# A two-layer hybrid step on one core: norm rows spread one product later, pools that wait by tile, and the samples' queries on four column tiles of 32 rows

## The chip, the cores and the metric

The kernel runs on one core of a Trainium2 chip. The metric is the device time of one execution in microseconds, the median of several runs. The engines are PE (TensorE), DVE (VectorE), ACT (ScalarE), POOL (GpSimd) and SP (SyncE, which only issues transfers here).

## The reference

One step of a two-layer model for a prompt of 1024 tokens and for 8 samples of 8 new tokens each, which share the weights (1088 columns in all), with D = 1024:

```python
for l in range(2):
    h = rmsnorm(x, g_mix[l])
    if l == 0:   # 8 forget-gate heads of 64, 4 differential heads of 2 x 64
        y = attention(h)   # prompt: causal; sample: 2048 cached positions, gathered by a page table, and its 8 new ones
    else:
        y = lru_mixer(h)
    x = x + y
    h = rmsnorm(x, g_ffn[l])
    x = x + (gelu(conv(h @ wa)) * (h @ wb)) @ wd      # inner size 3072
y = rmsnorm(x, g_final)
# softmax of a sample: fox  q.k/8 + cq - ck        (8 heads)
#                      diff (p1 - lam * p2) @ v    (4 heads, two maps each)
```

All is float32. Dense products are split into high and low parts (three products in the type fp32r); the attention products of a sample and the prompt's value products run in plain float32. An rmsnorm scales a column (a token) by one number, the reciprocal root of its mean square; the kernel computes it per column and has to spread it over all 128 partitions.

## The kernel before, in words

Activations lie with features on partitions and tokens along the free dimension. The program is written stage by stage; a scheduler orders each engine's instructions by program order and by a timeline that it models, so an instruction may go ahead of an earlier one that is not ready. Only in the attention stage is the order of SP's transfers that of the program (`manual_schedule`).

**Projections** (`proj_chunk`, `proj_v`): query, key and value products. The last part, `proj_v`, is merged with the first 24 steps of the samples' attention.

**Attention.** `merge` interleaves two job lists: the prompt's (`unit_scores`, `unit_norm`, `unit_values`) and the samples' (`key_job`, `softmax_job`, `value_job`). For each sample there are eight key jobs and eight value jobs, and each loads two pages (2 x 512 KB) into one of five buffers `raw` (`RAW = 5`), issued by SP at L818. A key job multiplies zero-padded queries `wz` (128 x 64 per chunk c of two heads and per kind, fox or diff) with the keys: eight calls (L858) that write rows 0 to 63 (fox) or 64 to 127 (diff) of a bank. So scores stand in 128 rows: 64 rows fox, head by head, then 64 rows diff, map by map. A value job multiplies the transposed weights `pT` with the values: for each page one call per kind with 512 columns (L932). `end` (L937) scales the sum, and `end_sum` transposes it in four pieces (L944) and picks each head's columns. In the profile each of these plain float32 calls leaves two matmul records, so L858 has 1024 and L932 544.

**Pools.** A pool that is allocated where released ones lay waits until the whole of them is done, unless it is made by `new_pool`, which waits tile by tile. In the first half of the kernel (`attp`, `proj`, `projn`, `vev`, `evp`, `xp`, `flp`, `flc`, `wos`, `rop`, `sa1`, `sa`, `pr`, `pq`, `pa`) they are of the first kind.

**From a mixer to the feed-forward part** (`to_ffn`, called twice). `down` is the output product by Strassen-like sums; its last loop runs over the two column halves c of the second 544 columns: product `t1`, `over` (squares into `hacc`, L1107 and L1108), `end(0)` when c is 0, product `b22`, `over`, `end(1 + c)`. `end(u)` takes the norm's numbers of unit u in `row`: `rstd_cols` sums the squares over partitions on PE (L196) and runs three Newton steps on DVE (L199, L167 to L175, twelve small instructions), then `row_bcast` (PE transposes, L213, and an ACT copy, L1118) spreads them. `half1` scales and splits the operands of the first 544 columns (`b11`, `b21`), `half2` those of one quarter (`t1`, `t2`, `t3`, `t4`, `b22`: 44 DVE instructions). `next(up)` starts `ffn_up`, whose first part multiplies 12 weight chunks with `b11` and `b21` alone (L1211 to L1213, 24 records for each chunk and operand). L1366 to L1368 are the products of `down`, L136 the low parts of all splits.

Of the kernel before, what the change touches and what calls it, by code (L numbers as in the profile page):

```python
# [20 lines left out]
D = 1024  # L21
# [17 lines left out]
STB = 4  # L39
FINE = False  # L40
LEAD = 1
WRAW = 6
# [36 lines left out]
def hybrid_step(ctx: ExitStack, tc: tile.TileContext, xT, w_in, w_fl, w_v, w_out, w_gate, w_x, w_lout, w_ai, ffn_a, ffn_b,  # L79
# [220 lines left out]

    attp = tc.alloc_tile_pool(name="attp", bufs=1, side="right")
    qs = attp.tile([128, 2, 4, TS], F32, name="qs")
# [13 lines left out]
    def attention_consts():  # L316
        SP.dma_start(ptt, ptab)
        SP.dma_start(newm, cst[:, CST["newm"][0]:CST["newm"][1]])
        lamp = tc.alloc_tile_pool(name="lamp", bufs=1, side="right")
# [43 lines left out]
    open_w("wp0", 2, 2)  # L363
    proj = tc.alloc_tile_pool(name="proj", bufs=1)
    projn = tc.alloc_tile_pool(name="projn", bufs=1, side="right")
    vev = tc.alloc_tile_pool(name="vev", bufs=3)
    evp = tc.alloc_tile_pool(name="evp", bufs=2)

# [25 lines left out]
    n0 = Norm(proj, projn, [vcol("mixg", k) for k in range(KC)], V)  # L394
    xp = tc.alloc_tile_pool(name="xp", bufs=1)
    xs = [xp.tile([128, T], F32, name=f"xs{k}") for k in range(KC)]
# [14 lines left out]
    P0 = n0.pairs()  # L411
    flp = tc.alloc_tile_pool(name="flp", bufs=1)
    wfr = flp.tile([128, KC, H], F32, name="wfr")
# [6 lines left out]
    def cached_gates():  # L420
        flc = tc.alloc_tile_pool(name="flc", bufs=1)

# [130 lines left out]
    for h in range(H):  # L553
        SP.dma_start(cqc[h * NQ:h * NQ + NQ, :], bass.AP(tensor=cq_sc.tensor, offset=cq_sc.offset + h * TS, ap=[[1, NQ], [NQ, NB]]))
    S.copy(csel[0:16], csr)
    for i in range(2):
# [3 lines left out]
    cached_gates()  # L560
    wos = tc.alloc_tile_pool(name="wos", bufs=1)
    for j in range(4):
# [9 lines left out]
    wos.release()  # L572
    rop = tc.alloc_tile_pool(name="rop", bufs=1)
    cost = rop.tile([128, T], F32, name="cost")
# [219 lines left out]
    open_ps("psS", "right", ss=4)  # L794
    sa1 = tc.alloc_tile_pool(name="sa1", bufs=1, side="right")
    sa = tc.alloc_tile_pool(name="sa", bufs=2, side="right")

# [27 lines left out]
    def batch_start(bt):  # L825
        b = bt["b"]
        w = bt["w"] = wz[b % 2]
        for kind in range(2):
            for hp in range(2):
                rows = slice(hp * 64, hp * 64 + 64)  # L830
                o, step = (hp * 8, 80) if kind == 0 else (hp * 32, 72)
                S.copy(sub_ap(w[rows], kind * 256 + o, [[step, 4], [1, NQ]]), qs[rows, kind, :, b * NQ:(b + 1) * NQ])
# [33 lines left out]
    def softmax_job(bt):  # L866
        def new_keys():
            b, w, sx, mx = bt["b"], bt["w"], bt["sx"], bt["mx"]
            ps = bt["pn"] = bank("ss")
            bq = slice(b * NQ, (b + 1) * NQ)  # L870
            PE.matmul(ps[:, 0:NQ], csel, cmn[:, bq], start=True, stop=False, skip_group_check=True)
            for c in range(4):
                for kind in range(2):
                    PE.matmul(ps[64 * kind:64 * kind + 64, 0:NQ], w[:, kind, c, :], kn[:, kind, c, bq], start=False,
                              stop=(c == 3), skip_group_check=True)

# [18 lines left out]
    def value_job(bt, g, x):  # L895
# [27 lines left out]
        def mm():  # L923
            if x == 0 and late:
                turn()
            if g == 0 and x == 0:
                bt["po"] = bank("oo")
            pT, po = bt["pT", g], bt["po"]
            for jj in range(n2):
                for kind in range(2):  # L930
                    f = slice(64 * kind, 64 * kind + 64)
                    PE.matmul(po[f], pT[:rows, 2 * x + jj, f], jb["raw"][:rows, jj, kind],  # L932
                              start=(g == 0 and x == 0 and jj == 0), stop=(g == 4), skip_group_check=True)

        def end():
            bt["ob"] = sa.tile([128, 512], F32, name="ob", bufs=2)
            S.activation(bt["ob"], bt["po"], AF.Copy, scale=bt["rl"])  # L937

        def end_sum():
            b, ob = bt["b"], bt["ob"]  # L940
            bq = slice(b * NQ, (b + 1) * NQ)
            pt = bank("tt", (128, 4, 128))
            for c in range(4):
                PE.transpose(pt[:, c, :], ob[:, c * 128:(c + 1) * 128], ident)  # L944
            for hp in range(2):
                rows = slice(hp * 64, hp * 64 + 64)
                V.tensor_copy(mixs[rows, :, bq], sub_ap(pt[rows], hp * 8, [[144, 4], [1, NQ]]))
            V.tensor_reduce(ods[:, :, bq], sub_ap(pt, 64, [[136, 4], [1, NQ], [32, 2]]), axis=AX.X, op=OP.add)
        return [load] + [None] * (LEAD - 1) + [start] + [None] * (GAP - 1) + [mm] + ([end, end_sum] if g == 4 else [])

# [53 lines left out]
    with tc.manual_schedule(engines={SP.engine}):  # L1004
# [3 lines left out]
        close_w()  # L1008
        pr = tc.alloc_tile_pool(name="pr", bufs=1, side="right")
        pq = tc.alloc_tile_pool(name="pq", bufs=1)  # L1010
        pa = tc.alloc_tile_pool(name="pa", bufs=1)
        mrow = pq.tile([128, 512], F32, name="mrow", bufs=1)
# [79 lines left out]
    class UnitNorm:  # L1092


        def __init__(self, pool, pool2):
            self.pool, self.pool2, self.acc, self.count = pool, pool2, {}, {}

# [12 lines left out]
        def row(self, u):  # L1110
            s0, m = UNITS[u]
            nt = 5 if u == 0 else 3
            cols = rstd_cols(self.acc[u], nt, 1.0 / D)
# [5 lines left out]
            row_bcast(cols, nt, evac)  # L1119
            return rb  # L1120
# [81 lines left out]
    def ffn_up(l, ops, uv):  # L1202
# [134 lines left out]

    def down(src, act, sm, nj, x, dp, rp, done, end):

# [72 lines left out]
        for c in two:  # L1412
# [22 lines left out]
    def to_ffn(l, src, act, sm, nj, x_src):  # L1435
# [18 lines left out]
        def end(u):  # L1454
            nonlocal rest1
            if u == 0:
                ops.half1(x, g, nf.row(0))
            else:
                r = nf.row(u)
                if u == 2:  # L1460
                    nfp.release()
                    dp.release()
                    rp.release()
                    rest1 = new_pool(name=f"opr{l}1")
                    ops.open(1, rest1)
# [4 lines left out]
        down(src, act, sm, nj, x, dp, rp, done, end)  # L1470
        xpool.release()
# [318 lines left out]
```

## Time and profile before

| | |
|---|---|
| median of 3 runs | 3138.46 us (3134.02 to 3145.78) |
| the profiled execution | 3136.24 us, its span 3134.5 us |
| PE busy in the span | 2957.0 us (94%), 21141 matmuls |
| DVE busy | 2100.7 us (67%) |
| ACT busy | 1324.4 us (42%) |
| mean granted PE clock | 0.972 |
| moved | 646.96 MB, 206 GB/s |

Times in views count from the start of the span. A row of a timeline gives start and length of a group of instructions of one kind, in brackets the idle time of the engine before it and what ended that. A row of windows gives each engine's busy time and, in parentheses, its instructions, then the granted PE clock as a share of 2.4 GHz, the mean busy share of the 16 DMA engines and what they moved. A matmul's length holds its fill and drain, so lengths of neighbours overlap.

### The profile page before, as it was taken

What the parts mean: (1) busy time and instruction counts of PE and PEld (TensorE: products, weight loads), DVE (VectorE), ACT (ScalarE), POOL (GpSimd) and SP (SyncE); (2) the same over time, 40 slices, a digit from 0 to 9 for tenths busy, and PEclk for the clock granted to TensorE, in tenths of its full rate; (3) what the DMA queues carried; (4) which work ended last, traced back from release to release, by engine and by line L of the source; (5) the groups of instructions that cost most, each with busy time, mean ns of one, the idle gap of its engine ahead of it and who ended that gap; (6) DMA issues with size and microseconds to landing.
All of it is one profiled execution on the core that took longest, in us unless ns stands there. A gap on an engine that the chain in (4) does not pass through costs nothing. (4 is left out here: it accounts for less than half of the span.)

```text
span 3134.5 us, 58133 instructions
## 1 busy us (share of the span) xinstructions
PE 2957.0 (94%) x21141; PEld 2709.5 (86%) x21141; DVE 2100.7 (67%) x4435; ACT 1324.4 (42%) x2477; POOL 398.9 (13%) x817
## 2 busy tenths in 40 slices
PE   7989999999997899899999999999969999999997
PEld 6988856565577899899999999999969899999997
DVE  6563134443458679988856777768785998886567
ACT  4111234444445533343344555555454334344444
POOL 0100010000000112321200011211011222221000
PEclk8999999999998999999999999999979999999999
DMA  4878688898785456544586652325735664448566
GB/s 147 238 226 308 208 324 306 308 338 319 274 263 191 161 174 207 199 143 140 175 269 193 216 184 96 100 97 167 262 126 172 221 209 161 151 145 260 181 187 212
DMA packets 383473, 646.96 MB, mean 206 GB/s; under 512 B 40305, under 2 KB 210690, under 8 KB 381138
## 3 DMA queue, kind: packets, MB, share of 16 engines
q1 hardware_dynamic: 321234, 478.65, 47.6%
q0 software_dynamic: 41792, 141.52, 12.2%
q10 hardware_dynamic: 20160, 23.07, 2.2%
q8 instruction: 166, 2.72, 0.4%
q14 instruction: 121, 0.99, 0.1%
HBM read 476.15 MB, written 166.95 MB: 205 GB/s over the span
## 5 line engine op out<-in xcount | busy, mean ns | idle before, releaser
L1060 ACT CAST b_hi<-b_raw 128x512 fp32r<-128x512 f32 (+1 forms) x645 | 394.8, 616 | 599.7 <-PE mm L1367 236.7
L136 DVE TENSOR_TENSOR b_lo<-b_raw,b_hi 128x512 fp32r<-128x512 f32 (+1 forms) x645 | 439.0, 683 | 236.6 <-ACT b_hi L1060 231.8
L1367 PE MATMUL mm<-d_lo,b_hi 128*128 128x272 f32 x1848 | 526.3, 293 | 4.6 <-DVE d_lo L136 4.5
L1368 PE MATMUL mm<-d_hi,b_lo 128*128 128x272 f32 x1848 | 525.2, 293 | 0.0
L1366 PE MATMUL mm<-d_hi,b_hi 128*128 128x272 f32 x1848 | 479.5, 297 | 40.7 <-ACT d_hi L1360 31.7
L1366 PEld LDWEIGHTS mm<-d_hi,b_hi 128*128 128x128 f32 x1848 | 331.4, 195 | 46.5 <-ACT d_hi L1360 40.6
L1367 PEld LDWEIGHTS mm<-d_lo,b_hi 128*128 128x128 f32 x1848 | 356.5, 193 | 6.4 <-DVE d_lo L136 6.2
L1368 PEld LDWEIGHTS mm<-d_hi,b_lo 128*128 128x128 f32 x1848 | 355.1, 193 | 0.0
L136 DVE TENSOR_TENSOR d_lo<-d_raw,d_hi 128x544 fp32r<-128x544 f32 (+1 forms) x297 | 175.5, 594 | 56.4 <-ACT d_hi L1360 55.2
L1360 ACT CAST d_hi<-d_raw 128x544 fp32r<-128x544 f32 (+1 forms) x297 | 160.8, 543 | 106.4 <-DMA d_raw<-a_b 50.0
L1082 PE MATMUL mm<-hh,b_hi 128*128 128x364 f32 (+1 forms) x480 | 158.5, 331 | 3.7 <-ACT b_hi L1060 3.1
L1083 PE MATMUL mm<-hl,b_hi 128*128 128x364 f32 (+1 forms) x480 | 157.6, 330 | 0.0
L1084 PE MATMUL mm<-hh,b_lo 128*128 128x364 f32 (+1 forms) x480 | 151.3, 330 | 0.0
L160 PE MATMUL mm<-hh,w_hi 128*128 128x364 f32 (+1 forms) x384 | 127.9, 335 | 14.4 <-DVE ev L296 7.9
L932 PE MATMUL oo<-raw,pT 128*64 128x512 f32 (+1 forms) x544 | 138.6, 604 | 1.1 <-ACT pT L921 1.1
L1211 PE MATMUL mm<-b22h,b_hi 128*128 128x272 f32 x384 | 115.0, 299 | 24.4 <-DVE bt L1294 24.4
L858 PE MATMUL ss<-raw,wz 128*64 128x256 f32 x1024 | 137.4, 389 | 0.0
L1271 ACT ACTIVATE ft<-ft 128x544 f32<-128x544 f32 x96 | 63.9, 666 | 169.1 <-DVE ft L1270 168.9
L161 PE MATMUL mm<-hl,w_hi 128*128 128x364 f32 (+1 forms) x384 | 127.9, 335 | 1.6 <-DVE hl L254 1.6
L162 PE MATMUL mm<-hh,w_lo 128*128 128x364 f32 (+1 forms) x384 | 127.3, 333 | 0.0
L675 ACT ACTIVATE st<-st,nb 128x128 f32<-128x128 f32 (+7 forms) x128 | 98.1, 768 | 55.2 <-DVE nb L669 29.4
L1212 PE MATMUL mm<-b22l,b_hi 128*128 128x272 f32 x384 | 114.1, 297 | 0.0
(401 smaller groups left out, 8401.6 us busy)
## 6 DMA issues: line engine op xcount, KB each, us to landing
raw<-in_kc SPq DMA_DIRECT2D x128, 512.0 KB
raw<-in_vc SPq DMA_DIRECT2D x128, 512.0 KB
b_raw<-w_sum SPq DMA_DIRECT2D x174, 256.0 KB
b_raw<-in_ffn_d SPq DMA_DIRECT2D x168, 256.0 KB
b_raw<-in_ffn_a SPq DMA_DIRECT2D x144, 256.0 KB
a_t<-ts POOLq DMA_DIRECT2D x116, 272.0 KB, 4.0
b_raw<-in_ffn_b SPq DMA_DIRECT2D x96, 256.0 KB
d_raw<-a_t SPq DMA_DIRECT2D x87, 272.0 KB
```

The source lines that it names most:

```text
L136: (eng or V).tensor_tensor(out, x, hi, op=OP.subtract)
L160: PE.matmul(ps[:, :n], hi[:, k, :], rh[:, s:s + n], start=(k == order[0]), stop=False)
L858: PE.matmul(ps[64 * kind:64 * kind + 64], w[:, kind, c, :], jb["raw"][:, :, kind, c, :], start=False, stop=(c == 3), skip_group_check=True)
L932: PE.matmul(po[f], pT[:rows, 2 * x + jj, f], jb["raw"][:rows, jj, kind], start=(g == 0 and x == 0 and jj == 0), stop=(g == 4), skip_group_ ...
L1060: S.copy(hi, raw)
L1082: PE.matmul(ps[:, :n], hi, rh[:, s:s + n], start=(k == order[0]), stop=False)
L1083: PE.matmul(ps[:, :n], hi, rl[:, s:s + n], start=False, stop=False)
L1084: PE.matmul(ps[:, :n], lo, rh[:, s:s + n], start=False, stop=(k == order[-1]))
L1360: S.copy(rh, raw)
L1366: PE.matmul(p, wh[:, m, :], rh[:, s], start=(start and j == 0), stop=False, skip_group_check=True)
L1367: PE.matmul(p, wh[:, m, :], rl[:, s], start=False, stop=False, skip_group_check=True)
L1368: PE.matmul(p, wl[:, m, :], rh[:, s], start=False, stop=(j == nj - 1), skip_group_check=True)
```

## The change

1. `UnitNorm.row` is cut into `rms` (sums and Newton steps) and `spread` (transposes and copy). In `to_ffn`, `end(u)` takes `rms(u)`; unit 0 is spread (and `half1` done) in `end(1)`, unit 1 in `mid`, a new call between `t1` and `b22` of c = 1, and unit 2 in `end(2)` after a first part of `ffn_up`, which now yields after chunks 0 to 2 as well. The last norm of the kernel still takes `row`.
2. The pools named above are made by `new_pool`.
3. The samples' queries are laid out by chunk c in 32 rows (two fox heads of 8 rows, then one diff head's two maps of 8). `wz` is 128 x 32 per chunk and kind. A key job still has eight calls of 256 columns, each on 32 columns of the array; a value job has four calls of 256 columns for each page in place of two of 512. The sum is 256 columns wide and takes two transposes, not four. The constants `csel`, `cqc` and `lamc` follow the new rows; `lamc` is filled by four transfers of POOL in place of one DVE copy.

```diff
-        V.tensor_copy(lamc[96:128, 1:2], lamc[96:128, 0:1])
+        for c in range(4):
+            r = slice(32 * c + 24, 32 * c + 32)
+            G.dma_start(lamc[r, 1:2], lamc[r, 0:1])
...
-        t = sa1.tile([128, 2, 4, 64], F32, name=f"wz{i}")
+        t = sa1.tile([128, 2, 4, 32], F32, name=f"wz{i}")
...
-            for c in range(4):
-                for kind in range(2):
-                    PE.matmul(ps[64 * kind:64 * kind + 64], w[:, kind, c, :], jb["raw"][:, :, kind, c, :], start=False,
-                              stop=(c == 3), skip_group_check=True)
+            for kind in range(2):
+                for c in range(4):
+                    PE.matmul(ps[32 * c:32 * c + 32], w[:, kind, c, :], jb["raw"][:, :, kind, c, :], start=False,
+                              stop=(kind == 1), tile_position=(0, 32 * c), skip_group_check=True)
...
-                for kind in range(2):
-                    f = slice(64 * kind, 64 * kind + 64)
-                    PE.matmul(po[f], pT[:rows, 2 * x + jj, f], jb["raw"][:rows, jj, kind],
+                for c in range(4):
+                    f = slice(32 * c, 32 * c + 32)
+                    PE.matmul(po[f, 0:256], pT[:rows, 2 * x + jj, f], jb["raw"][:rows, jj, :, 128 * c:128 * c + 128],
...
-            for c in range(4):
-                PE.transpose(pt[:, c, :], ob[:, c * 128:(c + 1) * 128], ident)
+            for kind in range(2):
+                PE.transpose(pt[:, kind, :], ob[:, kind * 128:(kind + 1) * 128], ident)
...
-        pr = tc.alloc_tile_pool(name="pr", bufs=1, side="right")
+        pr = new_pool(name="pr", bufs=1, side="right")
...
+            if f == NCOV:            # NCOV = 2, in ffn_up's first loop
+                yield
...
             if c == 0:
                 end(0)
+            elif mid:
+                mid()
             product("b22", ps, False, (c,))
...
         def end(u):
             nonlocal rest1
-            if u == 0:
-                ops.half1(x, g, nf.row(0))
-            else:
-                r = nf.row(u)
-                if u == 2:
...
-                    next(up)
-                ops.half2(x, g, r, u - 1)
+            if u == 1:
+                ops.half1(x, g, nf.spread(0))
+            nf.rms(u)
+            if u == 2:
...
+                next(up)
+                ops.half2(x, g, nf.spread(2), 1)
+                next(up)
+
+        def mid():
+            ops.half2(x, g, nf.spread(1), 0)
```

## Rows read from the trace of the kernel before

**Rows 1.** Windows of the whole kernel by engine: the samples' jobs beside `proj_v` (285 to 400 us), and beside the prompt's attention (400 to 898 us).
```profile
285.00:400.00 115.00, 115.00 (x893) 91.47 (x893) 10.77 (x25) 21.59 (x39) 1.46 (x3) 1.00 0.69 249
400.00:898.00 498.00, 494.48 (x3060) 293.23 (x3059) 205.52 (x842) 217.58 (x496) 38.25 (x87) 0.99 0.86 310
```

**Rows 2.** Groups of instructions by line, the whole run: records, busy us, mean ns of one.
```profile
L932 PE MATMUL oo<-raw,pT 128*64 128x512 f32 (+1 forms) x544 | 138.6, 604 | 1.1 <-ACT pT L921 1.1
L858 PE MATMUL ss<-raw,wz 128*64 128x256 f32 x1024 | 137.4, 389 | 0.0
```

**Rows 3.** The same by line for 400 to 900 us.
```profile
L932 PE MATMUL oo<-raw,pT 128*64 128x512 f32 (+1 forms) x496 | 127.2, 604 | 1.1 <-ACT pT L921 1.1
L858 PE MATMUL ss<-raw,wz 128*64 128x256 f32 x800 | 108.9, 390 | 0.0
```

**Rows 4.** Timeline of PE around the first key job.
```profile
285.53 0.28 PE L493 MATMUL tt<-w_hi,hh 128*128 128x256 f32 x1
285.65 0.28 PE L494 MATMUL tt<-w_lo,hh 128*128 128x256 f32 x1
285.86 1.95 PE L858 MATMUL ss<-raw,wz 128*64 128x256 f32 x16
287.74 0.39 PE L495 MATMUL tt<-w_hi,hl 128*128 128x256 f32 x1
```

**Rows 5.** The same timeline cut to 0.03 us (285.85 to 285.88): the records of that job which run in this stretch.
```profile
285.86 0.44 PE L858 MATMUL ss<-raw,wz 128*64 128x256 f32 x2
```

**Rows 6.** The lines of key and value products, 400 to 898 us: shortest, median and longest record in ns, first and last start.
```profile
L858 PE MATMUL ss<-raw,wz x800: 379/379/689, 400.7 to 849.7; 128*64 128x256 f32 x160
L932 PE MATMUL oo<-raw,pT x496: 587/592/1056, 405.6 to 893.5; 128*64 128x512 f32 x155, 8*64 8x512 f32 x11
```

**Rows 7.** Timeline of PE, one sample's new keys: records of 8 columns.
```profile
314.77 0.64 PE L874 MATMUL ss<-kn,wz 128*64 128x8 f32 x16
```

**Rows 8.** Timeline of PE in the merged stage, around a key job.
```profile
600.32 0.43 PE L714 MATMUL tt<-pf,v 128*64 128x256 f32 x1
600.33 0.43 PE L858 MATMUL ss<-raw,wz 128*64 128x256 f32 x1
600.59 0.38 PE L714 MATMUL tt<-pf,v 128*64 128x256 f32 x1
600.60 2.09 PE L858 MATMUL ss<-raw,wz 128*64 128x256 f32 x15
```

**Rows 9.** Windows in the merged stage in which the transfers were dense: 35 us, and the densest window of 100 us.
```profile
500.00:535.00 35.00, 35.00 (x205) 21.35 (x204) 14.37 (x48) 13.76 (x29) 3.45 (x7) 1.00 1.04 406
...
500.00:600.00 100.00, 99.83 (x618) 59.92 (x617) 43.69 (x180) 45.21 (x104) 9.89 (x22) 1.00 0.93 347
```

**Rows 10.** What SP's queue waited for, 400 to 898 us: us in total, times, longest.
```profile
SPq L818 <- PE ss L858: 94.3, 30, 7.6
SPq L818 <- PE oo L932: 93.8, 37, 12.1
```

**Rows 11.** Windows around the first passage to the feed-forward part, and the whole of both passages.
```profile
980.00:1000.00 20.00, 13.43 (x91) 12.94 (x90) 18.04 (x48) 12.37 (x28) 4.28 (x8) 0.78 0.74 244
1000.00:1020.00 20.00, 9.48 (x53) 8.83 (x53) 18.28 (x47) 9.41 (x22) 1.08 (x2) 0.71 0.11 36
1020.00:1040.00 20.00, 13.33 (x88) 12.47 (x87) 19.12 (x50) 11.37 (x28) 3.22 (x6) 0.89 0.43 141
...
1060.00:1080.00 20.00, 20.00 (x162) 20.00 (x162) 11.31 (x24) 12.81 (x29) 4.18 (x11) 1.00 0.69 220
...
965.00:1113.00 148.00, 120.27 (x881) 118.19 (x880) 107.82 (x258) 78.03 (x181) 23.53 (x47) 0.88 0.50 162
2245.00:2393.00 148.00, 120.93 (x899) 119.75 (x898) 106.92 (x257) 79.74 (x187) 23.04 (x46) 0.88 0.53 169
```

**Rows 12.** What PE waited for, 980 to 1060 us: us in total, times, longest.
```profile
PE mm L213 <- DVE nr_y L175: 17.0, 3, 8.3
PE mm L196 <- DVE hacc L1108: 5.2, 1, 5.2
```

**Rows 13.** The same for 2260 to 2340 us.
```profile
PE mm L213 <- DVE nr_y L175: 21.0, 3, 12.3
```

**Rows 14.** Timeline of PE in the first passage: the norm's instructions.
```profile
988.11 1.17 PE L196 MATMUL mm<-ones,hacc 128*128 128x2 f32 x10
995.50 1.33 PE L213 MATMUL mm<-ident,nr_y 128*128 128x128 f32 x5 [6.22 <-DVE nr_y L175]
...
1010.93 0.90 PE L213 MATMUL mm<-ident,nr_y 128*128 128x128 f32 x3 [8.34 <-DVE nr_y L175]
```

**Rows 15.** What PE waited for, 190 to 290 us.
```profile
PE mm L160 <- DVE ev L296: 7.9, 1, 7.9
PE tt L493 <- ACT v_ev L499: 5.9, 1, 5.9
```

**Rows 16.** Timeline of ACT and its transfers, 274 to 276 us; `row` is a tile of the pool `pr`.
```profile
274.42 0.85 ACTq L603 DMA_DIRECT2D row<-nc_sc  x2
275.32 0.47 ACT L499 ACTIVATE v_ev<-tt,nr_y 64x256 f32<-64x256 f32 x1 [5.95 <-DMA kl_sc<-stl]
```

**Rows 17.** Timeline of DVE, 189 to 194 us; `sh` and `cost` are tiles of the pool `rop`, `o_raw` one of `wos`.
```profile
189.32 0.01 DVE L461 LOAD_MASK_SELECT sh<-ev  x1 [4.14 <-DMA wo_sum<-o_raw]
...
193.16 1.29 DVE L463 TENSOR_TENSOR ev<-ev,cost 128x1088 f32<-128x1088 f32 x1 [2.40 <-DMA cost<-in_cst]
```

More of the change, by code (lines that the diff above doesn't have):

```diff
@@ L40 @@
 FINE = False
+NCOV = 2
 LEAD = 1
@@ L298, in scaled @@
                 V.scalar_tensor_tensor(dst, in0=src, scalar=scalar, in1=r, op0=OP.mult, op1=OP.mult)
-    attp = tc.alloc_tile_pool(name="attp", bufs=1, side="right")
+    attp = new_pool(name="attp", bufs=1, side="right")
     qs = attp.tile([128, 2, 4, TS], F32, name="qs")
@@ L318, in attention_consts @@
         SP.dma_start(newm, cst[:, CST["newm"][0]:CST["newm"][1]])
-        lamp = tc.alloc_tile_pool(name="lamp", bufs=1, side="right")
+        lamp = new_pool(name="lamp", bufs=1, side="right")
         lraw = lamp.tile([128, 4, 64], F32, name="lraw")
@@ L363, in hybrid_step @@
     open_w("wp0", 2, 2)
[L364 to L367, printed above, removed]
+    proj = new_pool(name="proj", bufs=1)
+    projn = new_pool(name="projn", bufs=1, side="right")
+    vev = new_pool(name="vev", bufs=3)
+    evp = new_pool(name="evp", bufs=2)
     order = [it for kind in range(2) for it in
@@ L411, in hybrid_step @@
     P0 = n0.pairs()
-    flp = tc.alloc_tile_pool(name="flp", bufs=1)
+    flp = new_pool(name="flp", bufs=1)
     wfr = flp.tile([128, KC, H], F32, name="wfr")
@@ L553, in hybrid_step @@
     for h in range(H):
-        SP.dma_start(cqc[h * NQ:h * NQ + NQ, :], bass.AP(tensor=cq_sc.tensor, offset=cq_sc.offset + h * TS, ap=[[1, NQ], [NQ, NB]]))
-    S.copy(csel[0:16], csr)
+        SP.dma_start(cqc[32 * (h // 2) + 8 * (h % 2):32 * (h // 2) + 8 * (h % 2) + NQ, :], bass.AP(tensor=cq_sc.tensor, offset=cq_sc.offset + h * TS, ap=[[1, NQ], [NQ, NB]]))
+    S.copy(csel[0:16].rearrange("k (c a r) -> k c a r", c=4, a=2)[:, :, 0], csr[:, :64].rearrange("k (c r) -> k c r", c=4))
     for i in range(2):
@@ L560, in hybrid_step @@
     cached_gates()
-    wos = tc.alloc_tile_pool(name="wos", bufs=1)
+    wos = new_pool(name="wos", bufs=1)
     for j in range(4):
@@ L572, in hybrid_step @@
     wos.release()
-    rop = tc.alloc_tile_pool(name="rop", bufs=1)
+    rop = new_pool(name="rop", bufs=1)
     cost = rop.tile([128, T], F32, name="cost")
@@ L794, in hybrid_step @@
     open_ps("psS", "right", ss=4)
-    sa1 = tc.alloc_tile_pool(name="sa1", bufs=1, side="right")
-    sa = tc.alloc_tile_pool(name="sa", bufs=2, side="right")
+    sa1 = new_pool(name="sa1", bufs=1, side="right")
+    sa = new_pool(name="sa", bufs=2, side="right")
     mixs = sa1.tile([128, 4, TS], F32, name="mixs")
@@ L830, in batch_start @@
                 rows = slice(hp * 64, hp * 64 + 64)
-                o, step = (hp * 8, 80) if kind == 0 else (hp * 32, 72)
-                S.copy(sub_ap(w[rows], kind * 256 + o, [[step, 4], [1, NQ]]), qs[rows, kind, :, b * NQ:(b + 1) * NQ])
+                S.copy(sub_ap(w[rows], kind * 144 + hp * 8, [[32, 4], [1, NQ]]), qs[rows, kind, :, b * NQ:(b + 1) * NQ])
         bt["sx"] = sa.tile([128, PAST + NQ], F32, name="sx")
@@ L929, in mm @@
             for jj in range(n2):
-                for kind in range(2):
-                    f = slice(64 * kind, 64 * kind + 64)
-                    PE.matmul(po[f], pT[:rows, 2 * x + jj, f], jb["raw"][:rows, jj, kind],
-                              start=(g == 0 and x == 0 and jj == 0), stop=(g == 4), skip_group_check=True)
+                for c in range(4):
+                    f = slice(32 * c, 32 * c + 32)
+                    PE.matmul(po[f, 0:256], pT[:rows, 2 * x + jj, f], jb["raw"][:rows, jj, :, 128 * c:128 * c + 128],
+                              start=(g == 0 and x == 0 and jj == 0), stop=(g == 4), tile_position=(0, 32 * c), skip_group_check=True)
         def end():
             bt["ob"] = sa.tile([128, 512], F32, name="ob", bufs=2)
-            S.activation(bt["ob"], bt["po"], AF.Copy, scale=bt["rl"])
+            S.activation(bt["ob"][:, :256], bt["po"][:, :256], AF.Copy, scale=bt["rl"])
         def end_sum():
@@ L942, in end_sum @@
             pt = bank("tt", (128, 4, 128))
-            for c in range(4):
-                PE.transpose(pt[:, c, :], ob[:, c * 128:(c + 1) * 128], ident)
+            for kind in range(2):
+                PE.transpose(pt[:, kind, :], ob[:, kind * 128:(kind + 1) * 128], ident)
             for hp in range(2):
                 rows = slice(hp * 64, hp * 64 + 64)
-                V.tensor_copy(mixs[rows, :, bq], sub_ap(pt[rows], hp * 8, [[144, 4], [1, NQ]]))
-            V.tensor_reduce(ods[:, :, bq], sub_ap(pt, 64, [[136, 4], [1, NQ], [32, 2]]), axis=AX.X, op=OP.add)
+                V.tensor_copy(mixs[rows, :, bq], sub_ap(pt[rows], hp * 8, [[32, 4], [1, NQ]]))
+            V.tensor_reduce(ods[:, :, bq], sub_ap(pt, 144, [[32, 4], [1, NQ], [8, 2]]), axis=AX.X, op=OP.add)
         return [load] + [None] * (LEAD - 1) + [start] + [None] * (GAP - 1) + [mm] + ([end, end_sum] if g == 4 else [])
@@ L1095, in __init__ @@
         def __init__(self, pool, pool2):
-            self.pool, self.pool2, self.acc, self.count = pool, pool2, {}, {}
+            self.pool, self.pool2, self.acc, self.count, self.cols = pool, pool2, {}, {}, {}
         def square(self, k, x, u):
@@ L1336, in ffn_up, with down @@
         yield
-    def down(src, act, sm, nj, x, dp, rp, done, end):
+    def down(src, act, sm, nj, x, dp, rp, done, end, mid=None):
         u = [dp.tile([128, NH], F32, name=f"du{m}") for m in range(4)]
@@ L1455, in end @@
             nonlocal rest1
-            if u == 0:
-                ops.half1(x, g, nf.row(0))
-            else:
-                r = nf.row(u)
-                if u == 2:
[L1461 to L1465, printed above, removed]
-                    next(up)
-                ops.half2(x, g, r, u - 1)
+            if u == 1:
+                ops.half1(x, g, nf.spread(0))
+            nf.rms(u)
+            if u == 2:
+                nfp.release()
+                dp.release()
+                rp.release()
+                rest1 = new_pool(name=f"opr{l}1")
+                ops.open(1, rest1)
+                next(up)
[3 more added lines that the diff above has]
+            ops.half2(x, g, nf.spread(1), 0)
         rest1 = None
         up = ffn_up(l, ops, uv)
-        down(src, act, sm, nj, x, dp, rp, done, end)
+        down(src, act, sm, nj, x, dp, rp, done, end, mid)
         xpool.release()
```

23 lines of the change are left out of this document (13 added, 10 removed).

## The prediction

> **What bounds the kernel now.** I read the page's busy shares first, then windows by stage, then in each stage the lines and waits of the engine that is full. From 285 to 898 us the samples' jobs run, and PE is the full engine: it is busy for all of the first 115 us and for 494.5 of the next 498, at full clock, while DVE and ACT are under half busy [rows 1]. The transfers move 310 GB/s there, and dense stretches reach 406 [rows 1, 9], so they are near their limit without setting the pace: SP stood for 94.3 and 93.8 us waiting for PE to free a page buffer [rows 10]. What is worth something here is PE time. In the two passages to the feed-forward part PE is not full. At full pace 20 us hold 162 records; from 980 to 1040 they hold 91, 53 and 88, and DVE is busy for 18 to 19 us of each 20 [rows 11]. At that pace the 881 and 899 records of the two passages would take 109 and 111 us of 148 each [rows 11], so 39 and 37 us are lost to waits and to the clock (0.88 granted on average). Newton steps are the named wait for 17.0 and 21.0 of them [rows 12, 13].
>
> **Part 1, the queries by chunk.** A key job is 16 records in 1.95 us [rows 4]. A stretch of 0.03 us already holds two of them [rows 5]: the two 64-column tiles run side by side. The first record takes 0.43, so the other seven pairs come (1.95 - 0.43) / 7 = 0.217 us apart, 0.108 a record. 1024 records [rows 2] make 1024 x 0.108 = 111 us. A value record takes 592 ns against 379 for half the columns [rows 6], 213 more, so its pairs come 0.217 + 0.213 = 0.43 us apart, and 272 pairs [rows 2] make 117 us. Together 228 us of PE; the lines show 276 busy [rows 2], since fill, drain and mode changes are in it.
>
> After it there are 1024 + 1088 records of 256 columns on four tiles. If four run side by side as two do now, that is 2112 / 4 x 0.217 = 114 us, so 114 are saved. If only two do, nothing is. No row has more than two tiles at work, so these are the ends. Issue is no limit: records of 8 columns come (0.64 - 0.20) / 15 = 0.03 us apart, below the 0.054 that four tiles need [rows 7]. I take four, because the pair of a job starts together [rows 5] and nothing between two and four shows a limit. By window: 800 and 496 of the records lie after 400 us [rows 3], which gives 800 x 0.054 + 248 x 0.215 = 97 us there and 17 before.
>
> The Trainium skill, "TensorE: Matmul & The Clock Gate" (section "Measured speedup vs the span model"), gives 2.38 for three column tiles, 0.79 a tile. Worked out from that page, as an estimate, four tiles do 3.2 times one tile's work, and the sum would save 84 us in place of 114; no run here shows three or four yet.
>
> Entering this mode costs time: from L494 to the key job it takes 0.21 us where such records are 0.12 apart, and the way out (287.43 to 287.74) 0.31 where pairs are 0.217 apart, so 0.09 each way [rows 4]. These changes exist today. New are those against L714 on 64 columns, now a neighbour in the same mode; the two stand interleaved record by record, three changes for one meeting [rows 8]. The ends are none and both sides of all 136 jobs, 24 us. I take 6, since most jobs meet products on 128 columns. Sixteen transposes fall away, 2 us.
>
> Not all of it arrives. From 400 us on PE alone would need 498 - 97 + 6 - 2 = 405 us. The bytes, 310 x 498 = 154 MB, need 380 us at 406 GB/s and 445 at the 347 of the densest 100 us [rows 1, 9]. So PE stays the bound by a little, and the slack that SP has in its waits [rows 10] shrinks by half. Page loads, the next heads' loads and waits on ACT's exponentials, hidden so far, are what is late next. I put 20 us for them, between none and the 40 of the 445. The stage falls by 97 - 6 + 2 - 20 = 73; I take 70. From 285 on the transfers have room (249 GB/s [rows 1]) and the partner is dense `proj_v` work: of 17 I take 15.
>
> The small edits cost nothing: `lamc` is filled by POOL, which is busy for 1.5 us of the 115 before 400 [rows 1], and its reader comes after 400; if that cover were gone, four issues would be 2 us. ACT's copy of 256 columns in place of 512 is off the path.
>
> **Part 2, the norm rows.** Today PE takes the sums, waits 6.22 us for the Newton steps, spreads, and then waits 8.34 for the next unit's steps, which stand behind `half1` on DVE [rows 14]; the third wait is the rest of 17.0. After it a product stands between. The first gap can be filled: the next product's splits are already made. The third is covered by 120 records of `ffn_up`, 120 x 20 / 162 = 15 us, against the rest of 2.4. The second hardly can, because DVE is full there and `half1`, Newton steps and `half2` stay as many; they are only ordered otherwise, and PE waits for splits instead. The 5.2 for `hacc` stays [rows 12]. What is late next is DVE. So I take 10 us a passage, 20 in all, between nothing and the newton and `hacc` waits of both (17.0 + 5.2 + 21.0 = 43).
>
> **Part 3, the pools.** At 270 us ACT holds two loads of `row`, a tile of a pool that waits for the whole of a released one, and PE loses 5.9 us [rows 15, 16]; at 195 it loses 7.9, in part since `rop` waits for all of `wos` [rows 15, 17]. Tile by tile some of that goes. Bounds: 14 us gained, or 6 lost if a load that may go earlier blocks an in-order queue the same way. I take 6.
>
> **The sum.** 70 + 15 + 20 + 6 = 111 us off the profiled execution's 3136.2 gives 3025; the median stands 2.2 above that execution, so 3027.
>
> **The rivals.**
> - *Transfers set the pace* of the merged stage. For it: 0.86 busy and 1.04 in dense stretches [rows 1, 9]. Against: SP's 188 us of waiting [rows 10]. At 347 GB/s the stage takes 445 us and gives 53 in place of 70; with bursts that starve PE 30. Time 3044 to 3067.
> - *Only two tiles run side by side*, because each call's two records go to one tile one after the other and the queue does not reach past them. Against: calls of one job start in pairs from the first record on [rows 5], where a strict order would start with a single one. But two calls show no reach over four. Then part 1 costs 6 and saves 2 (3142) and the rest gives 26: 3116, between 3112 and 3142. The Trainium skill, "TensorE: Matmul & The Clock Gate" (section "The mechanism"), says that matmuls start and end strictly in program order, which would make this case; the pair that starts together [rows 5] disagrees with it unless the records are interleaved in the queue.
> - *Slower*: tiles of 32 columns don't overlap at all, each record waiting for the one before. Place: L858 and L932. Price: 2112 x 0.217 = 458 us against 228, so 3027 + 85 + 230 = 3342. It decides from a mean distance of (228 + 26 - 6) / 2112 = 0.117 us a record on. Nothing shows it; against it, tiles of 64 overlap.
> - *The norm rows give nothing*, since DVE is full: 3047. That lies inside the forecast's range.
>
> **The numbers.** The forecast with four tiles and PE as the bound: 0.66. Transfers as the bound: 0.14. Two tiles only: 0.14. No overlap: 0.06. The low end takes the upper bounds, 97 + 17 + 30 + 10 off: 2985. The high end takes in the transfers' case with 30 + 13 and nothing from norms and pools, 3095. That leaves out the last two cases, 0.2. A measurement of this kernel can tell about 0.5% (16 us) from no change. Two tiles only falls half on either side of 3123. So faster 0.66 + 0.14 + 0.07 = 0.87, same 0.07, slower 0.06.
>
> **What would show it.** Right: L858 and L932 with records of about 379 ns, four of them in a 0.03 us stretch, a key job in about 1.1 us in place of 1.95; the merged stage near 428 us, with 350 to 370 GB/s and SP's waits on L858 and L932 about halved; `proj_v`'s stretch near 100 us; no wait for `nr_y` over 3 us in the passages, but waits for `d_lo` or `b_lo` in their place; the ACT wait at 270 us gone. Wrong: pairs of records 0.217 us apart as before; PE waiting for `raw`; newton waits of the old length; or the stage no shorter because ACT or DVE chains have taken PE's place.

## The result and the profile after

The changed kernel takes 3017.8 us (median; 3011.5 to 3020.8), the kernel before 3140.7 beside it: the ratio is 0.9607 [0.9582, 0.9632], 123 us off. The forecast was 3027. The profiled execution of after has a span of 3014.8 us, 119.7 less than before's, at the same mean granted clock (0.972).

The windows of after answer to [rows 1] and [rows 9]: the samples' jobs beside `proj_v`, the whole merged stage, and two of its four full stretches of 100 us. The two first rows hold as many records, but not the same work: in after more value products lie ahead of 400 us, so gains are read from where a stage ends.

```profile
285.00:378.50 93.50, 93.29 (x893) 78.03 (x885) 11.05 (x27) 20.24 (x37) 2.52 (x5) 1.00 0.82 299
378.80:815.00 436.20, 410.27 (x3554) 251.47 (x3546) 206.16 (x851) 218.77 (x500) 37.09 (x85) 0.96 0.97 356
...
500.00:600.00 100.00, 94.27 (x834) 57.05 (x822) 50.33 (x203) 52.16 (x122) 9.63 (x22) 0.97 1.01 375
...
700.00:800.00 100.00, 94.43 (x811) 56.48 (x808) 50.39 (x210) 50.45 (x112) 5.50 (x14) 0.95 0.90 330
```

The merged stage, from the last `proj_v` record to the first product of `down`, lasted 501.5 us before (400.6 to 902.1) and lasts 436.2 now (378.8 to 815). PE is no longer full in it: 25.9 us idle, where it was 5.1. The transfers run at 356 GB/s in place of 310.

The timeline around one of the first key jobs answers to [rows 4], and the same cut to 0.04 us (284.23 to 284.27) to [rows 5]. Sixteen records take 1.07 us in place of 1.95, and four of them stand where two stood.

```profile
284.24 1.07 PE L860 MATMUL ss<-raw,wz 128*32 128x256 f32 x16
285.24 0.39 PE L496 MATMUL tt<-w_hi,hh 128*128 128x256 f32 x1
```

```profile
284.24 0.42 PE L860 MATMUL ss<-raw,wz 128*32 128x256 f32 x4
```

The two lines over the whole run, records, busy us and mean ns, answer to [rows 2]: 154.5 us busy together, where it was 276.0.

```profile
L934 PE MATMUL oo<-raw,pT 128*32 128x256 f32 (+1 forms) x1088 | 84.1, 393 | 2.5 <-DMA raw<-out_o_dv 1.6 <-ACT pT L923 0.9
L860 PE MATMUL ss<-raw,wz 128*32 128x256 f32 x1024 | 70.4, 394 | 2.5 <-DMA raw<-in_kc 2.5
```

What SP's queue waited for from 378.8 to 815 us answers to [rows 10]. The two waits for PE are halved; new are 39 us of waits for earlier transfers of pages.

```profile
SPq L821 <- PE ss L860: 49.6, 28, 6.2
SPq L821 <- PE oo L934: 45.9, 28, 7.3
SPq L821 <- DMA raw<-in_vc: 23.4, 17, 3.4
...
SPq L821 <- DMA raw<-in_kc: 15.6, 6, 6.8
```

What PE waited for in the same stretch: a list of short waits with no one head.

```profile
PE tt L733 <- DVE st L701: 4.9, 5, 3.3
PE ss L655 <- DVE mx L659: 3.3, 7, 0.7
PE ss L655 <- DMA qk<-qk_sc: 3.0, 1, 3.0
```

The first passage in windows of 20 us answers to [rows 11], and PE's waits in it (815 to 1000 us) to [rows 12]; behind them those of the second passage (2059 to 2250 us), for [rows 13].

```profile
895.00:915.00 20.00, 16.85 (x130) 15.96 (x128) 19.00 (x51) 12.01 (x27) 6.45 (x12) 1.00 0.90 295
915.00:935.00 20.00, 14.16 (x74) 13.01 (x73) 19.39 (x40) 12.55 (x26) 1.18 (x3) 0.74 0.29 89
935.00:955.00 20.00, 20.00 (x162) 19.88 (x161) 19.30 (x58) 13.68 (x38) 4.31 (x9) 1.00 0.55 181
955.00:975.00 20.00, 17.88 (x142) 17.48 (x141) 19.35 (x55) 13.25 (x36) 3.16 (x6) 1.00 0.50 162
```

```profile
PE mm L1375 <- ACT d_hi L1369: 6.0, 3, 5.5
PE mm L1376 <- DVE d_lo L137: 5.4, 4, 4.3
PE mm L214 <- DVE nr_y L176: 3.3, 2, 2.4
```

```profile
PE mm L1375 <- ACT d_hi L1369: 11.6, 2, 5.9
PE mm L214 <- DVE nr_y L176: 8.2, 1, 8.2
```

The 80 us around the norms as a whole, of before and then of after:

```profile
980.00:1060.00 80.00, 52.27 (x338) 50.19 (x337) 71.50 (x191) 44.43 (x107) 11.27 (x21) 0.79 0.39 130
```

```profile
895.00:975.00 80.00, 68.89 (x502) 66.33 (x501) 77.04 (x201) 51.49 (x126) 15.09 (x28) 0.94 0.56 182
```

DVE is at least as full as before, 77.0 us of the 80 where it was busy for 71.5. Yet PE does 502 records beside it in place of 338. The `hacc` wait of 5.2 us is gone, and 17.0 us of Newton waits are 3.3. In the second passage one of 8.2 is left. The waits for `d_hi` are those of before (5.6 and 11.8 us there).

Step by step, from one profiled execution of each kernel. Executions that keep one order of instructions on PE differ by 6 to 7 us in such stretches (`p_alone` below), so less than that is no answer.

| stretch | before, us | after, us | difference | forecast |
|---|---|---|---|---|
| start to the last `proj_v` record | 400.5 | 378.7 | -21.8 | -15 and the pools' -6 |
| merged stage | 501.5 | 436.2 | -65.3 | -70 |
| first passage, and `ffn_up` behind it | 666.4 | 647.4 | -19.0 | -10 |
| second passage, and `ffn_up` behind it | 683.0 | 667.0 | -16.0 | -10 |
| the rest | 883.1 | 885.5 | +2.4 | 0 |

### The profile page after: what moved, and what is told of

The parts are those of the page before. It is cut to its first block, busy times and chain, and to the rows that moved or that the text cites. A ratio compares the mean times of both kernels' runs of the same rounds, so it can differ in the third digit from the quotient of the medians.

```text
span 3014.8 us, 59153 instructions
## 1 busy us (share of the span) xinstructions
PE 2848.4 (94%) x21669; PEld 2650.6 (88%) x21669; DVE 2098.2 (70%) x4434; ACT 1321.9 (44%) x2477; POOL 408.4 (14%) x821
## 5 line engine op out<-in xcount | busy, mean ns | idle before, releaser
L1218 PE MATMUL mm<-b22h,b_hi 128*128 128x272 f32 x384 | 114.6, 299 | 20.8 <-DVE bt L1301 20.8
L1220 PE MATMUL mm<-t2h,b_lo 128*128 128x272 f32 x384 | 108.6, 289 | 5.8 <-DVE b_lo L137 5.8
L1220 PE MATMUL mm<-b22h,b_lo 128*128 128x272 f32 x384 | 113.7, 296 | 0.0
```

What stands on the lines that cost most here:

```text
L1220: PE.matmul(p[:, :NT], lo[:, k, :], rh, start=False, stop=(k == 3), skip_group_check=True)
```

## The experiments

The theory: four column tiles run side by side and free PE time, part of which goes to new short waits; the norm rows' new order fills waits of PE with products that are ready; the pools do little. The rivals: transfers set the pace of the merged stage; the queue doesn't reach over four tiles; the gain of the passages belongs to the pools.

### Each part alone

`q_alone` is part 3 of the change, `n_alone` part 1, `p_alone` part 2, each on the kernel before.

```diff
  p_alone, sixteen pools in all, one of them (`lamp`) not named above:
-    attp = tc.alloc_tile_pool(name="attp", bufs=1, side="right")
+    attp = new_pool(name="attp", bufs=1, side="right")
```

Expected of `q_alone`: 

> The queries on four column tiles alone, with the norm rows and the pools of before. Theory (four tiles run side by side, PE sets the pace, transfers take a little of it back): the last value record came 79 us earlier in the kernel after, 22 of them before 400 us, and some of the 22 are the pools'. So 78 to 86 us off, about 3057 where the kernel before takes 3140; last L932-like record near 820 us of the span, key job about 1.07 us. Rival (part of the attention's gain is the pools', which let loads come earlier through the whole stage): 60 to 70 us off, and the pools alone over 12.

Expected of `n_alone`: 

> The norm rows' change alone (rms and spread apart, one product later, and the pause of the up projection after two chunks), on the kernel before. Theory (the milestones of the two kernels: about 16 us gained in each of the two passages): 28 to 34 us off, about 3110. Rival (my forecast's step: 10 a passage, DVE is full): 20 off, 3120. Rival (the passages gain because of pools that no longer wait as a whole): 10 to 20 off here, and the rest with the pools alone.

Expected of `p_alone`: 

> Only the pools are changed to those that wait tile by tile, on the kernel before. Theory: the two gaps of PE at 195 and 270 us shrink (7.9 to 5.6 and 5.9 to 2.4 in the kernel after), so 5 to 8 us off, about 3133, and nothing in the passages. Rival (pools matter for the later stages): over 12 off, with the gain behind 900 us.

Measured, beside 3137.8 for before: `q_alone` 3068.3, ratio 0.978 [0.9756, 0.9804]; `n_alone` 3107.7, 0.9898 [0.9879, 0.9917]; `p_alone` 3144.4, 1.0014 [1.0001, 1.0026]. That is -70, -30 and +7, together -93 where the whole change gives -123. `n_alone` is as its theory has it: the forecast's 20 lies outside its interval (26 to 38 us), and the rival that the passages gain by the pools, with 10 to 20 here, is out. `p_alone` misses the 5 to 8 us that were expected of it. `q_alone` falls short of the 78 to 86 expected. Yet its first product of `down` starts at 814.7 us, as in after (814.9), so the attention's gain of 87 us is the queries' alone and not the pools'; some 17 of them are lost again behind it. The parts don't add up, so the next two take one part back from the kernel after.

### Each part taken back

`old_norms` is after with part 1 undone, `old_pools` after with part 2 undone.

```diff
  old_norms, beside the old row():
         def end(u):
             nonlocal rest1
-            if u == 1:
-                ops.half1(x, g, nf.spread(0))
-            nf.rms(u)
+            if u == 0:
+                ops.half1(x, g, nf.row(0))
...
```

Expected of `old_norms`: 

> The kernel after with the norm rows of before (queries and pools as after). If the parts add up: the norm rows alone gave 30, so 30 on top of 3018, 3048. If the norm rows are worth more beside the other parts (the parts alone came to 93 where all together gave 123): up to 57, 3075. By the profiled stages of the kernels with and without them (means 649.7 against 669.7 us from the first down product to the end of the first up projection, 669.3 against 686.6 in the second layer): 37, 3055. My forecast's step: 20, 3038.

Expected of `old_pools`: 

> The kernel after with the pools of before (queries and norm rows as after). If the pools give nothing or cost a little as they did alone: 3010 to 3020. If they are what makes the whole more than its parts: 3035 to 3045. My forecast's step: 6, 3024.

`old_norms` takes 3066.5 (0.9771 [0.9753, 0.9789]), so beside the new queries the norm rows are worth 49 us (51 by the ratios). `old_pools` takes 3024.6 (0.9624 [0.9605, 0.9644]), where the forecast's step would put it, but its interval overlaps that of after.

The pools leave PE's order of instructions as it was: in the traces `p_alone` has that of before, `old_norms` that of `q_alone`, `old_pools` that of after, and only the waits differ. With the new pools the three pairs differ by +0.14%, -0.09% and -0.18%: of both signs, and inside the intervals but for the first, which leaves out zero by 0.01%. The profile has a trace of them. The wait of PE at 270 us is 5.9 in before [rows 15] and 6.1 in `old_pools`, but 3.6 in `p_alone` and 2.4 in after; the other one of those rows has not shrunk (7.9 and 5.0 with the old pools, 9.1 and 5.6 with the new). So the pools are worth 2 to 4 us in one wait and nothing that the runs can tell from zero in the time.

Where do the norm rows gain? Windows over a passage and the part of `ffn_up` behind it, first and second layer, of before, `old_norms` and after. The first two numbers are the length and PE's busy time.

```profile
902.10:1568.50 666.40, 616.79 (x4750) 612.12 (x4749) 545.52 (x1117) 275.33 (x519) 133.82 (x269) 0.96 0.55 181
2164.00:2847.00 683.00, 631.19 (x4902) 627.60 (x4901) 559.74 (x1113) 284.10 (x532) 136.51 (x280) 0.96 0.56 181
```

```profile
817.10:1486.60 669.50, 619.57 (x4754) 614.46 (x4751) 545.50 (x1114) 276.84 (x520) 135.82 (x269) 0.95 0.55 180
2082.00:2773.50 691.50, 635.12 (x4901) 631.68 (x4900) 560.98 (x1113) 285.03 (x532) 135.67 (x280) 0.95 0.55 179
```

```profile
814.90:1462.30 647.40, 616.09 (x4753) 611.09 (x4751) 545.83 (x1114) 274.39 (x520) 131.99 (x269) 0.97 0.57 186
2059.00:2726.00 667.00, 627.37 (x4899) 624.00 (x4898) 558.41 (x1113) 284.25 (x532) 142.98 (x280) 0.98 0.57 185
```

From `old_norms` to after the two stretches lose 22.1 and 24.5 us, 46.6 in all. PE's idle time (length less busy) falls from 49.9 to 31.3 and from 56.4 to 39.6, 35.4 together. Its busy time, for the same records to within 4 in the counts, falls by 3.5 and 7.8: that part goes with the granted clock, 0.95 against 0.97 and 0.98. The named waits of `old_norms`, first passage (817 to 1000 us) and second (2082 to 2300), of which those for `nr_y`, `hacc` and `t2h` went or shrank, while `d_hi` keeps 11.6 us in after:

```profile
PE mm L213 <- DVE nr_y L175: 16.8, 3, 8.4
PE mm L196 <- DVE hacc L1109: 6.5, 1, 6.5
```

```profile
PE mm L213 <- DVE nr_y L175: 21.1, 3, 12.3
PE mm L1367 <- ACT d_hi L1361: 13.4, 2, 7.7
PE mm L1367 <- ACT t2h L1147: 5.5, 1, 5.5
```

Where the queries' gain loses its 17 us is not shown. With the same old norm rows the two stretches are 3.1 and 8.5 us longer in `old_norms` than in before. But `p_alone`, whose order on PE is that of before, has them 6.1 and 6.8 us longer in its one profiled execution:

```profile
896.90:1569.40 672.50, 621.01 (x4750) 615.60 (x4749) 545.21 (x1117) 275.71 (x518) 133.58 (x269) 0.95 0.55 179
2167.20:2857.00 689.80, 633.57 (x4902) 629.17 (x4901) 560.00 (x1114) 284.27 (x532) 135.30 (x280) 0.96 0.55 179
```

So that difference needs no other order of instructions, and why the norm rows give 49 here and 30 alone stays open.

### The norm rows, unit by unit

```diff
  early0:
-            if u == 1:
-                ops.half1(x, g, nf.spread(0))
             nf.rms(u)
+            if u == 0:
+                ops.half1(x, g, nf.spread(0))
  no_mid:
             nf.rms(u)
+            if u == 1:
+                ops.half2(x, g, nf.spread(1), 0)
...
-        down(src, act, sm, nj, x, dp, rp, done, end, mid)
+        down(src, act, sm, nj, x, dp, rp, done, end)
  third_old:
-NCOV = 2
+NCOV = 11
...
             if u == 2:
+                r2 = nf.spread(2)
...
-                ops.half2(x, g, nf.spread(2), 1)
+                ops.half2(x, g, r2, 1)
```

Expected of `early0`: 

> The kernel after, but unit 0's spread and half1 stand at the end of its own product again, behind its Newton steps; the third unit's order and the pause of the up projection stay. Theory: the first waits of the two passages (6.2 us in the first passage of before, and as much in the second) come back, and clock with them: 14 to 20 on top of 3018. Rival: DVE is full and only the order differs, so the wait moves to the splits: within 5 us.

`early0` takes 3023.1 (0.9628 [0.9609, 0.9646]). It answers another question than it was made for: in the trace PE's instructions stand in the very order of after. So where unit 0's spread is written doesn't matter here, and the run is a second measure of after: 5.3 us by the medians (6.6 by the ratios) is what two measures of one order can differ by. What unit 0's late spread is worth by itself was not measured.

Expected of `no_mid`: 

> The kernel after, but half2 of unit 1 follows unit 1's Newton steps at once instead of one product later. Theory: the second wait (8.3 us in the first passage of before) comes back in both passages: 16 to 22 on top of 3018. Rival (my forecast's step: this gap can hardly be filled because DVE is full, so nothing was gained by moving it): within 5 us.

`no_mid` takes 3056.8 (0.9737 [0.9721, 0.9753]), 39 more than after, twice the 16 to 22 expected. Its two stretches take 669.9 and 681.7 us, for 647.4 and 667.0. PE's waits in both passages (818 to 1000 and 2085 to 2290 us):

```profile
PE mm L214 <- DVE nr_y L176: 14.9, 2, 8.4
...
PE mm L197 <- DVE hacc L1110: 2.9, 1, 2.9
```

```profile
PE mm L214 <- DVE nr_y L176: 17.9, 2, 12.3
```

The Newton waits are back at their length of before, both that of unit 1 (8.4, 12.3) and that of unit 0 (14.9 - 8.4 = 6.5 and 17.9 - 12.3 = 5.6), since in this trace unit 0's spread stands right behind its sums again. So the 39 us are the price of both waits, not of unit 1's alone. The rival, that a full DVE leaves nothing to gain there, is refuted.

Expected of `third_old`: 

> The kernel after with the third unit as before: its spread stands right behind its Newton steps, and half2 of it follows all 12 chunks of the up projection's first part, not three of them. If the parts of the norm rows add up (49 for all of them, 39 of that when only the second unit is put back): about 10 on top of 3018, with a wait for hacc near 5 us and one for nr_y of 2.4 back in each passage. My forecast's step: this wait is worth 2.4 a passage at most and the 5.2 for hacc was there to stay, so 0 to 5. Two executions of one instruction order have differed by 5 us, so less than that is no answer.

`third_old` takes 3048.0 (0.9702 [0.9684, 0.9719]), 30 more than after, against 10 and 0 to 5 expected. Its row of PE's timeline behind the first passage:

```profile
960.41 0.88 PE L214 MATMUL mm<-ident,nr_y 128*128 128x128 f32 x3 [16.46 <-DVE nr_y L176]
```

No wait for `hacc` came back; the wait for `nr_y` has grown. Unit 2's Newton steps stand among and behind unit 1's `half2` on DVE and end at 960.3 us, in `third_old` as in after. But here PE stands for 16.5 us before unit 2's spread, with products of `ffn_up` queued behind it; in after the spread stands behind the first chunks, and PE does 144 of these products between unit 2's sums and its spread. 39 and 30 add up to 69, more than the 49 of the whole: each of the two edits alone leaves most of the loss, and the gain needs both.

### How far TensorE reaches in its queue

```diff
  tile_order, in the key jobs; the value jobs likewise (c, then jj):
-            for kind in range(2):
-                for c in range(4):
+            for c in range(4):
+                for kind in range(2):
```

Expected: 

> The kernel after with the loops of the two jobs turned about: the two calls on one column tile come one behind the other (four records on the same tile in a row), where the kernel after goes to the next tile with each call. Same records, same tiles, same bytes. If PE reaches over many queued records: a key job stays near 1.07 us and the time within 5 us of 3018. If it starts a record only beside its near neighbours in the queue, the key job goes toward 1.5 to 1.95 us and PE's stage gets 40 to 85 us longer: 3055 to 3100. If strict order held, so that only a call's last record and the next call's first meet, it would be over 3100.

Measured 3044.1 (0.9698 [0.9678, 0.9718]), 26 more than after. The key job in the timeline, whole and cut to 0.06 us (281.86 to 281.92), and the two lines:

```profile
281.87 1.09 PE L860 MATMUL ss<-raw,wz 128*32 128x256 f32 x16 [0.16 <-DMA raw<-in_kc]
```

```profile
281.87 0.45 PE L860 MATMUL ss<-raw,wz 128*32 128x256 f32 x4 [0.16 <-DMA raw<-in_kc]
```

```profile
L934 PE MATMUL oo<-raw,pT 128*32 128x256 f32 (+1 forms) x1088 | 102.3, 396 | 3.9 <-DMA raw<-in_vc 1.7 <-DMA raw<-out_o_dv 1.6 <-ACT pT L923 0.6
L860 PE MATMUL ss<-raw,wz 128*32 128x256 f32 x1024 | 72.3, 392 | 1.3 <-DMA raw<-in_kc 1.3
```

The key job keeps its length, and four records still start within 0.06 us, though by the order of the calls the first records of neighbouring tiles are now four records apart, where in after they are two. So a record does not wait for those of other tiles ahead of it, and starts are not in strict order, unless the queue holds a call's records in another order than that of the calls. The time lies between the first two expectations: the key job is as the first has it, but the value line costs 18.2 us more, and the merged stage is 18.3 longer (454.5).

Why the values pay for this order and the keys don't can be read from the edit and the timeline. A key call reads both pages of its job, a value call one of them. With c outside, the second call of a value job is the first that reads the second page, and there the job is cut in two. A value job between the same products, first in after, then in `tile_order`:

```profile
453.82 0.64 PE L934 MATMUL oo<-raw,pT 128*32 128x256 f32 x8
...
456.21 0.64 PE L934 MATMUL oo<-raw,pT 128*32 128x256 f32 x8
```

```profile
453.13 0.62 PE L934 MATMUL oo<-raw,pT 128*32 128x256 f32 x2
...
455.49 1.08 PE L934 MATMUL oo<-raw,pT 128*32 128x256 f32 x14
```

Two records on one tile take about as long as eight on four, so this job costs 1.70 us in place of 1.28. After has 69 pieces of 8 records, `tile_order` 38 of 2 and 33 of 14; 33 times 0.42 makes 14 of the 18 us, as an estimate. Value jobs that are not cut take 1.09 us in `tile_order`, like its key jobs.

### What still costs the merged stage

```diff
  half_after; half_before is the same on the kernel before:
-        for jj in range(2):
+        for jj in range(1):
...
-    jb["raw"][:, :, kind, c, :]
+    jb["raw"][:, 0:1, kind, c, :].to_broadcast([128, 2, 128])
...
-    jb["raw"][:rows, jj, :, 128 * c:128 * c + 128]
+    jb["raw"][:rows, 0, :, 128 * c:128 * c + 128]
  raw6:
-RAW = 5
+RAW = 6
```

Expected of `half_after`: 

> The kernel after, but only one of the two pages of a job is loaded and TensorE reads it twice: the job's records are the same, the pages' bytes fall by half (part of the cache is left out). If transfers expose about 20 us of the merged stage, as the forecast put it: 12 to 25 us off, 2993 to 3006. If PE alone sets the pace: within 5 us of 3018. If transfers set the pace outright (the rival): over 30 off.

Expected of `half_before`: 

> The same leaving out of one page in two, on the kernel before. PE is full in its merged stage (494.5 of 498 us), so every theory here expects little: 0 to 5 us off 3140. If more than 10 comes off, the transfers already cost PE something that its busy time does not show.

Expected of `raw6`: 

> The kernel after with six page buffers in place of five. If the exposed transfers are bursts that a deeper queue smooths: 3 to 10 us off. If the stage is bound by PE or by the bytes as a whole: within 3 us of 3018.

`half_after` takes 3017.1 (0.9604 [0.9578, 0.963]), as after; `half_before` 3146.8 (1.0026 [1.0014, 1.0038]), not faster than before. So the 12 to 25 us that the forecast's step would have given did not come. The merged stage of `half_after`:

```profile
379.80:809.00 429.20, 414.96 (x3557) 261.57 (x3556) 204.91 (x846) 217.88 (x500) 37.40 (x86) 0.97 0.68 231
```

With 231 GB/s in place of 356 the stage is 7 us shorter, and PE is still idle for 14.2; SP's waits for PE to free a buffer rise to 119.6 and 114.1 us. So of the 25.9 us of idle time in after, about 7 to 12 belong to the pages' transfers, and the rest to waits on DVE, ACT and other loads. That is an estimate from one execution, whose order of instructions is another one. The rival that transfers set the pace is out.

`raw6` takes 3035.7 (0.9657 [0.964, 0.9674]), 18 more than after; both theories expected it no slower. Its merged stage:

```profile
378.80:831.00 452.20, 417.82 (x3554) 253.77 (x3547) 202.59 (x845) 218.35 (x500) 37.59 (x85) 0.95 0.94 345
```

PE is idle for 34.4 us there, in many short waits for DVE and ACT (6.6 for `st` the largest) and one of 5.6 us for which the profile names no cause. The scheduler's order of instructions is another one with six buffers. Which of its differences costs the 16 us of the stage was not tried.

## Why the prediction was right, and where its steps were off

**Four column tiles: right in mechanism and size.** The distance of the groups, (1.07 - 0.42) / 3 = 0.217 us, is that of the pairs before, with four records in each. Nothing was lost per tile from two tiles to four, so the sum's 114 us was the right term: the two lines lost 121.5 us of busy time. The lower estimate from the Trainium skill, "TensorE: Matmul & The Clock Gate" (section "Measured speedup vs the span model"), was not: its 2.38 for three tiles does not carry over to four tiles of two records a call here. The rival of 3116, that two records on one tile hold up the next tile's, fell with the four records that start together, and with `tile_order`. With it the rule of the Trainium skill's same page, section "The mechanism", a strict order of starts, does not fit these runs, unless the queue holds a call's records in another order than that of the calls.

**The merged stage: 65 for 70.** The terms behind it were near. PE's busy time fell by 496.4 - 410.3 = 86 against a net 93 (97, less 6, plus 2). Part of the difference goes with the clock, 0.96 granted for 0.99; the 6 us for changes of mode were not measured by themselves. 20.8 us of idle time came back where 20 had been put. But what fills them was put too much on the transfers: `half_after` leaves them 7 to 12, the rest is a scatter of waits on DVE and ACT. Ahead of the stage 21.8 us came off for 21, and that this sum came out is luck: the pools' 6 are not needed for it, because `q_alone` has 21.6 without them. Some 4 us of it can be spread between executions: in `n_alone`, with the queries and pools of before, the last `proj_v` record starts at 396.5, in before at 400.2.

**What the sum left out** is that the parts act on each other: the queries alone give 70 of the 87 us that the attention gains, and the norm rows 30 alone but 49 beside the new queries. The cause stays open.

**The norm rows: the failed step.** "The second hardly can, because DVE is full there" put 10 us a passage where 19.0 and 16.0 came against before (22.1 and 24.5 against `old_norms`). DVE is full in after too. Yet PE is held up by DVE only while it has nothing else that is ready, and what stands in front on DVE was changed. In before unit 1's `half2` (1012.3 to 1037.4 us) ran beside the last products of `down`, with their splits and the squares for `hacc` between its instructions. In after `down` and those squares are done before `half2` starts (939.7 to 959.2), and beside it PE has products of `ffn_up`, which need only what `half1` makes. Of the records in the 80 us, 294 are `ffn_up`'s where 149 were; `down`'s are 173 and 153. `no_mid`, in which the waits of units 0 and 1 both come back, is 39 us slower. The forecast's "the 5.2 for `hacc` stays" failed with it: the wait is gone in after, and 2.9 of it are back in `no_mid`. That waits for `d_lo` would come in place of Newton's was right (5.4 us in the first passage, 2.2 before). "No Newton wait over 3 us" holds in the first (2.4) and not in the second (8.2). The upper bound of 43 for both passages holds against before (35) and not against `old_norms` (46.6); 11 us of the latter are records that run at the higher clock, which the bound left out.

**The pools: 6 forecast, which the runs can't tell from nothing.** `p_alone` is 7 us slower than before. `old_pools` is 7 slower than after by the medians, but so, by 5, is `early0`, which has the new pools and after's order. One wait of PE fell by 2 to 4 us, the other didn't.

So the forecast was 9 us off because errors nearly cancel: by the table the passages gave 35 for 20, the merged stage 65 for 70, and the start its 21 without the pools.

## What to carry to other kernels

Plain float32 products with few output rows took about half the time here on four column tiles that they took on two, where the calls on different tiles were not cut apart. Look then at what was hidden behind them, since of the 86 us freed in one stage 21 came back as short waits. A full engine is no proof that a wait for it can't be filled: ask which ready work stands behind the waiting instruction in the other engine's queue, and move the wait behind it. Where a scheduler orders the program, read from the trace whether an edit changed the order at all (`early0` did not), and judge two edits that move one chain together.

## What the chip showed that was not expected

- Four matmul records on four column tiles start within 0.04 us, and still within 0.06 us when the first ones of neighbouring tiles are four records apart in the order of the calls (`tile_order`).
- The granted clock fell behind a single short wait. These windows of after show the stretch before, in and behind a wait of 2.98 us for `qk`: the granted clock is 1.00 before it (2.4 GHz) and 0.50 (1.2 GHz) for the next 6.6 us, in which 29 records ran where the stretch before had 126 in 12 us (other products in part).

```profile
570.00:582.00 12.00, 12.00 (x126) 7.08 (x126) 5.01 (x19) 5.68 (x15) 1.55 (x3) 1.00 1.01 379
582.30:585.20 2.90, 0.00 (x0) 0.00 (x0) 2.68 (x10) 0.69 (x1) 0.00 (x0) 1.00 1.04 372
585.40:592.00 6.60, 6.52 (x29) 5.13 (x30) 2.31 (x16) 4.34 (x13) 0.83 (x3) 0.50 1.03 407
```

- A sixth page buffer made the kernel slower by 18 us (0.6%), in another order of instructions. SP waited less for earlier transfers of pages (19.3 us for 39), PE more for DVE and ACT.
